# Branch C's pairs prepared on VectorE and ScalarE, with b and k of both heads in the same slots

## The chip, the cores and the metric

The kernel runs on one core of a Trainium2 chip. Its metric is the device time of one execution in microseconds, as the median of several runs. The engines are named as the profile names them: PE (matrix multiply), DVE (VectorE), ACT (ScalarE), POOL (GpSimd) and SP (it issues the DMAs).

## The reference, cut to what matters

A trunk of two layers over 640 tokens (128 context, 512 latent) has three parallel mixers A, B and C. The change touches C alone, a bidirectional delta-rule scan over 8 heads of 64 channels.

```python
def _wkv_scan(s0, r, w, k, v, a_vec, b_vec, reverse):
    def step(state, inp):
        r_t, w_t, k_t, v_t, a_t, b_t = inp
        sa = jnp.einsum('bhij,bhj->bhi', state, a_t)
        state = (state * w_t[:, :, None, :] + sa[..., None] * b_t[:, :, None, :]
                 + v_t[..., None] * k_t[:, :, None, :])
        y_t = jnp.einsum('bhij,bhj->bhi', state, r_t)
        return state, y_t
...
    for d, s0 in ((0, s0_f), (1, s0_b)):
        w_raw = w0[d] + jnp.tanh(wd[:, :, d]) @ w_up[d]
        decay = jnp.exp(-jnp.exp(-jax.nn.softplus(-w_raw) - 0.5))
        a = jax.nn.sigmoid(a0[d] + ad[:, :, d] @ a_up[d])
        k_d = hd(k * (1.0 + (a - 1.0) * k_a))
        s_fin, y_d = _wkv_scan(s0.astype(f32), rh, hd(decay), k_d, vh, -kk, kk * hd(a), reverse=(d == 1))
        bonuses.append(jnp.sum(rh * k_d * r_k, axis=-1, keepdims=True) * vh)
```

## The kernel before

The scan is done in chunks of 64 tokens, ten of them, in two directions. Heads are taken in pairs: a pair p holds 128 channels, head 0 on partitions 0 to 63 and head 1 on partitions 64 to 127, so a layer has four pairs and the kernel eight. A pair goes through these stages:

- `c_prep` (preparation). For each direction d, ACT makes tanh of the decay and of the gate (`lw`, `ta`, line 516), DVE scales the decay (517) and runs its cumulative sum (519), ACT takes exponentials in both signs (`TP`, `TM`, 525), DVE makes `kd` (533, 535) and `b2` (538). Then come eight products, for each head one of each kind on 64 partitions: `b2` times a decay table into `BK` (547, DVE), `kkn` times a table into `L1` (549, DVE), `kd` times a table into `BK` (551, POOL) and `xr` times a table into `L1` (552, POOL). In `BK` the slot of b is the head's number and the slot of k the other one.
- `c_pairs`. PE multiplies `BK` by `L1` of a head for each chunk (`pA`, 611); DVE masks one half of the partitions (614) and ACT copies the other (616), POOL masks that copy (619 to 624). PE then transposes `BK` (`pb`, 631) and ACT copies it back (632).
- `c_inverse`. Sixty small steps on DVE (658, 660) between transposes (652, 662, 670), then small matmuls on PE (`px` 679, `py` 691).
- `c_bonus`, then `c_scan` with ten dependent chunk steps among PE, ACT, DVE and POOL, `c_gn` (a norm per head; its two equal products at 830 stand one on DVE and one on POOL) and `c_out`.

While pair p is scanned, the preparation, the pairs and the inverse of pair p + 1 and the projections of the other mixers ("fillers": matmuls of 320 columns, `pcm`, lines 225 to 227, with weights split into two parts by ACT at 174 and by DVE or POOL at 175) are recorded in between, at a rate from the table `PLAN`. A scheduler then sets the final order of each engine's queue from its own estimate of times, and each engine works through its queue in that order. The transposed `BK` of a pair, `BT` in the scan, is multiplied by `VZ`, in which head 0's values stand on the second half of the partitions and head 1's on the first.

Of the kernel before, what the change touches and what calls it, by code (L numbers as in the profile page):

```python
# [10 lines left out]
F32 = mybir.dt.float32  # L11
# [96 lines left out]
class Trunk:  # L108
    def __init__(self, ctx, tc, I, O):
# [30 lines left out]
        G.memset(self.nhalf, -0.5)  # L140
        self.sc2 = sc = cst.tile([128, KT, 2], F32, tag="sc", name="sc")
# [297 lines left out]
    def c_prep(self, l, p, x, ps):  # L439
# [61 lines left out]
        for d in range(2):  # L501
# [15 lines left out]
            V.tensor_scalar(out=lw, in0=lw, scalar1=-HK, scalar2=-HK, op0=ALU.mult, op1=ALU.add)  # L517
# [10 lines left out]
            else:  # L528
# [4 lines left out]
            V.tensor_scalar(out=kd, in0=ta, scalar1=self.ka2[:, p:p + 1], scalar2=self.ka1[:, p:p + 1],  # L533
                            op0=ALU.mult, op1=ALU.add)
# [5 lines left out]
            def v3(ap, h):  # L540
                return ap[PR[h]].rearrange("p (c s) -> p c s", s=64)


            fl = (slice(None), slice(None, None, -1))[d]
            for h in range(2):
                r_ = PR[h]
                V.scalar_tensor_tensor(out=BK[r_, us, h, fl], in0=v3(b2, h), scalar=0.5,
                                       in1=tB[r_, :, oB:oB + 64], op0=ALU.mult, op1=ALU.mult)
                V.scalar_tensor_tensor(out=L1[h][r_, us, 0, fl], in0=v3(kkn, h), scalar=-1.0,
                                       in1=tA[r_, :, oA:oA + 64], op0=ALU.mult, op1=ALU.mult)  # L550
                G.tensor_tensor(out=BK[r_, us, 1 - h, :], in0=v3(kd, h), in1=tB[r_, :, oB:oB + 64], op=ALU.mult)
                G.tensor_tensor(out=L1[h][r_, us, 1, :], in0=v3(xr, h), in1=tR[r_, :, oR:oR + 64], op=ALU.mult)
# [3 lines left out]
    def c_bonus(self, e, xv, ps):  # L556

        V, S, G, PE = self.V, self.S, self.G, self.PE
        p, cs = e.p, self.cs
        prod = self.tmp("prod")[:, 0:T]  # L560
        G.tensor_tensor(out=prod, in0=e.kds[0], in1=e.kds[1], op=ALU.add)
        V.scalar_tensor_tensor(out=prod, in0=prod, scalar=self.cv[:, CV_RK + p:CV_RK + p + 1], in1=e.xr,
                               op0=ALU.mult, op1=ALU.mult)
        ph, pl = (self.ct.tile([128, 660], F32R, tag="tmp", name=n)[:, 0:T] for n in ("prh", "prl"))
        self.split(ph, pl, prod)
        bonus = self.tmp("bonus")[:, 0:T]
        for half in range(2):
            hs = slice(half * H, half * H + H)
            pb = ps.tile([128, 512], F32, tag="g", name="pbn")
            PE.matmul(pb[:, 0:H], lhsT=self.bones_r, rhs=ph[:, hs], start=True, stop=False)  # L570
            PE.matmul(pb[:, 0:H], lhsT=self.bones_r, rhs=pl[:, hs], start=False, stop=True)
            V.tensor_tensor(out=bonus[:, hs], in0=pb[:, 0:H], in1=xv[:, hs], op=ALU.mult)
        self.nc.sync.dma_start(out=self.bsp[p], in_=bonus)
# [17 lines left out]
    def c_pairs(self, e, ps):  # L591
# [12 lines left out]
        for d in range(2):  # L604
            for h in range(2):
                for c0, n in ((0, 4), (4, 4), (8, 2)):
                    us = slice(10 * d + c0, 10 * d + c0 + n)
                    pA = pc("pA")
                    for j in range(n):
# [4 lines left out]
                    V.tensor_tensor(out=L1[h][QR[h], us].rearrange("p u a s -> p u (a s)"), in0=pv[QR[h]],  # L614
                                    in1=self.amask[QR[h], d:d + 1, :].to_broadcast([64, n, 128]), op=ALU.mult)
                    S.copy(out=AB[PR[h], us], in_=pv[PR[h]].rearrange("p u (a s) -> p u a s", a=2))  # L616
# [11 lines left out]
        for u0 in range(0, 20, 4):  # L628
# [3 lines left out]
            S.copy(out=BK[:, u0:u0 + 4].rearrange("p u a s -> p (u a s)"), in_=pb)  # L632
# [173 lines left out]
    def c_gn(self, l, e):  # L806
# [22 lines left out]
        for x, en in enumerate((V, G)):  # L829
            en.tensor_tensor(out=e.yt[:, :, x], in0=sqy, in1=lnx.to_broadcast([128, 10, 64]), op=ALU.mult)  # L830
# [794 lines left out]
```

## Time and profile before

| what | us |
|---|---|
| median of 3 runs | 2320.77 |
| lowest and highest of them | 2318.45, 2337.36 |
| the profiled execution | 2325.66 |
| its span on the core | 2323.9 |
| PE busy | 2130.8 |
| DVE busy | 1589.3 |
| ACT busy | 1108.1 |
| POOL busy | 690.2 |

The profile is one execution. Its span is what the views cover; 1.8 us of the profiled execution lie around it. An engine's busy time is the union of its instructions' durations; a PE that is busy is not a PE at its peak. A row that gives a mean mixes hindered and unhindered instructions; the least and the median tell them apart.

### The profile page before, as it was taken

Reading aid. Unit: us, or ns where it says so; the run is one execution under the profiler, and the core shown is the slowest. Engines: PE = TensorE matmul, PEld = TensorE weight load, DVE = VectorE, ACT = ScalarE, POOL = GpSimd, SP = SyncE. Lnnn points to the kernel's source line nnn. Section 1 sums busy time; section 2 is a strip of 40 time slices with the busy share of each in tenths; the row PEclk is TensorE's granted clock in tenths of the full one; section 3 lists DMA queues with packets and bytes.
Section 4 is the critical chain, followed back from the end, with each engine's and each line's share of the span. In section 5 each row is a group of like instructions: output and inputs, shape, how many; then the busy total and the mean of one; then the engine's idle time right before and its main releaser. Section 6 shows DMA issues by size and latency. Waiting matters only on the chain.

```text
span 2323.9 us, 40367 instructions
## 1 busy us (share of the span) xinstructions
PE 2130.8 (92%) x15380; PEld 2016.8 (87%) x15380; DVE 1589.3 (68%) x3062; ACT 1108.1 (48%) x2462; POOL 690.2 (30%) x761
## 2 busy tenths in 40 slices
PE   8899998999789889989989999999898889999898
PEld 6889998998789778879988999999898777888898
DVE  4676877867845676775648668668677568667673
ACT  4444443544443666662354444434443447667333
POOL 3332527335233221102033133253352332210011
PEclk9999989989899999999999999899797999999899
DMA  6232222222223311126612322222123231110562
GB/s 227 77 102 77 78 73 95 73 93 84 88 91 109 100 38 52 39 77 192 200 53 74 102 73 79 76 94 76 58 74 99 67 101 46 46 55 24 174 191 83
DMA packets 111762, 209.70 MB, mean 90 GB/s; under 512 B 14416, under 2 KB 33488, under 8 KB 111568
## 3 DMA queue, kind: packets, MB, share of 16 engines
q1 hardware_dynamic: 111568, 207.12, 28.1%
q8 instruction: 121, 1.98, 0.4%
q14 instruction: 73, 0.60, 0.1%
HBM read 163.52 MB, written 43.55 MB: 89 GB/s over the span
## 4 chain that ended last, share of the span: by engine, by line
PE 65%; DVE 18%; ACT 7%; DMA 4%; issue 4%; POOL 2%; DVEq 0%; SPq 0%; ACTq 0%; POOLq 0%
PE pcm L225 10%; PE pcm L226 10%; PE pcm L227 10%; PE sc L958 3%; PE sca L767 2%; PE pm L178 2%; PE pm L179 2%; PE pm L180 2%; DVE wlo L175 2%; PE pA L611 2%; PE pp L973 2%; PE px L679 1%; DVE nm L961 1%; PE scb L782 1%; ACT whi L174 1%
## 5 line engine op out<-in xcount | busy, mean ns | idle before, releaser
L225 PE MATMUL pcm<-hh,whi 128*128 128x320 f32 x1952 | 636.0, 326 | 21.7 <-DVE modc L252 6.7
L227 PE MATMUL pcm<-hh,wlo 128*128 128x320 f32 x1952 | 626.1, 321 | 13.7 <-DVE wlo L175 13.6
L226 PE MATMUL pcm<-hl,whi 128*128 128x320 f32 x1952 | 625.9, 321 | 0.0
L225 PEld LDWEIGHTS pcm<-hh,whi 128*128 128x128 f32 x1952 | 381.3, 195 | 29.4 <-DVE modc L252 7.9
L227 PEld LDWEIGHTS pcm<-hh,wlo 128*128 128x128 f32 x1952 | 380.2, 195 | 18.0 <-DVE wlo L175 16.9
L174 ACT CAST whi<-wraw 128x512 fp32r<-128x512 f32 (+1 forms) x356 | 226.6, 666 | 331.3 <-PE pcm L226 122.0
L226 PEld LDWEIGHTS pcm<-hl,whi 128*128 128x128 f32 x1952 | 381.5, 195 | 1.5
L175 DVE TENSOR_TENSOR wlo<-wraw,whi 128x512 fp32r<-128x512 f32 (+1 forms) x262 | 224.4, 871 | 95.1 <-ACT whi L174 91.3
L175 POOL TENSOR_TENSOR wlo<-wraw,whi 128x512 fp32r<-128x512 f32 x94 | 124.1, 1337 | 195.1 <-ACT whi L174 171.1
L778 POOL COPY ubd<-VZ 64x128 f32<-64x128 f32 x160 | 68.0, 425 | 328.1 <-ACT VZ L775 291.1
L164 DVE TENSOR_TENSOR pl<-pp,ph 128x512 fp32r<-128x512 f32 x160 | 108.4, 685 | 47.8 <-ACT ph L163 46.7
L178 PE MATMUL pm<-yh,whi 128*128 128x320 f32 x384 | 121.7, 317 | 7.1 <-DVE OT L995 3.0
L163 ACT CAST ph<-pp 128x512 fp32r<-128x512 f32 x160 | 92.4, 587 | 64.5 <-PE pp L973 53.9
L961 DVE TENSOR_REDUCE nm<-sc 128x1 f32<-128x640 f32 x128 | 104.4, 818 | 25.0 <-PE sc L958 23.6
L179 PE MATMUL pm<-yl,whi 128*128 128x320 f32 x384 | 121.3, 316 | 0.0
L180 PE MATMUL pm<-yh,wlo 128*128 128x320 f32 x384 | 121.0, 315 | 0.0
L963 ACT ACTIVATE P<-sc,nm 128x640 f32<-128x640 f32 x128 | 102.0, 798 | 18.7 <-DVE nm L961 14.4
L973 PE MATMUL pp<-small,P 128*128 128x128 f32 x640 | 102.2, 280 | 7.2 <-ACT P L963 4.3
L973 PEld LDWEIGHTS pp<-small,P 128*128 128x128 f32 x640 | 80.9, 144 | 24.9 <-ACT P L963 5.3
L611 PE MATMUL pA<-L,BK 128*128 128x128 f32 x640 | 90.7, 285 | 11.4 <-ACT AB L616 7.8
L767 PE MATMUL sca<-VZ,L 128*128 128x64 f32 x640 | 93.3, 285 | 7.7 <-DVE VZ L799 7.6
L996 POOL TENSOR_TENSOR OT<-OT,z 128x640 f32<-128x640 f32 x16 | 27.8, 1736 | 239.7 <-DVE OT L995 216.2
(375 smaller groups left out, 5021.6 us busy)
## 6 DMA issues: line engine op xcount, KB each, us to landing
wraw<-in_win SPq DMA_DIRECT2D x156, 256.0 KB, 2.9
wraw<-in_wg SPq DMA_DIRECT2D x96, 256.0 KB, 3.1
wraw<-in_wmod SPq DMA_DIRECT2D x64, 256.0 KB, 2.9
gsp<-gt SPq DMA_DIRECT2D x48, 320.0 KB, 3.1
gt<-gsp SPq DMA_DIRECT2D x48, 320.0 KB, 3.4
wraw<-in_wo SPq DMA_DIRECT2D x24, 512.0 KB, 4.4
cm<-gsl SPq DMA_DIRECT2D x26, 320.0 KB, 2.5
wraw<-in_wmod SPq DMA_DIRECT2D x16, 512.0 KB, 6.5
```

Of the source, the lines that this page charges most:

```text
L174: self.S.copy(out=hi[part], in_=raw)
L175: sub.tensor_tensor(out=lo[part], in0=raw, in1=f32(hi[part]), op=ALU.subtract)
L178: self.PE.matmul(out, lhsT=lh, rhs=rh, start=first, stop=False)
L179: self.PE.matmul(out, lhsT=lh, rhs=rl, start=False, stop=False)
L180: self.PE.matmul(out, lhsT=ll, rhs=rh, start=False, stop=last)
L225: PE.matmul(p[0:m, 0:H], lhsT=wh[:, kt], rhs=self.hh[:, kt, rs], start=(kt == 0), stop=False)
L226: PE.matmul(p[0:m, 0:H], lhsT=wh[:, kt], rhs=self.hl[:, kt, rs], start=False, stop=False)
L227: PE.matmul(p[0:m, 0:H], lhsT=wl[:, kt], rhs=self.hh[:, kt, rs], start=False, stop=(kt == KT - 1))
L611: PE.matmul(pA[:, j * 128:(j + 1) * 128], lhsT=BK[:, u].rearrange("p a s -> p (a s)"), rhs=L1[h][:, u].rearrange("p a s -> p (a s)"), star ...
L767: PE.matmul(a4[:, d, h], lhsT=L1[h][:, uu[d]].rearrange("p a s -> p (a s)"), rhs=VZ[h][:, cc[d], :], start=(h == 0 and d == 0), stop=False ...
L961: V.tensor_reduce(out=nm, in_=sc[:, :, 0:H], axis=AX.XY, op=ALU.max, negate=True)
L973: PE.transpose(p[:, qt * 128:(qt + 1) * 128], Ps[qt][:, t * 128:(t + 1) * 128], ident)
```

## The change

The four POOL products of a direction go. `kd` and `xr` are multiplied on DVE. In `BK` slot 0 now holds b and slot 1 holds k for both heads, so b and k each take one product on 128 partitions in place of two on 64. The scale and offset of `lw` and of `kd` (before 517 and 533) become ACT activations. In `c_pairs` the halves of `pA` are now the same for both heads, so for head 1 the copies cross partitions. The transposed `BK` needs its halves exchanged for head 1, so the one ACT copy at 632 becomes three: two on ACT and one on DVE. The sum of the two `kd` in `c_bonus` goes from POOL to DVE. In `c_gn` the second, equal product becomes an ACT copy of the first.

```diff
--- before.py
+++ after.py
@@ -138,6 +138,8 @@
         G.memset(self.ones, 1.0)
         self.nhalf = cst.tile([128, 16], F32, tag="nhalf", name="nhalf")
         G.memset(self.nhalf, -0.5)
+        self.nhk = cst.tile([128, 1], F32, tag="nhk", name="nhk")
+        G.memset(self.nhk, -HK)
         self.sc2 = sc = cst.tile([128, KT, 2], F32, tag="sc", name="sc")
         self.S.activation(out=sc, in_=self.cT, func=AF.Tanh, scale=0.5)
         V.scalar_tensor_tensor(out=sc, in0=sc, scalar=1.0, in1=self.cT, op0=ALU.add, op1=ALU.mult)
@@ -514,7 +516,7 @@
                         PE.matmul(pw[:, 0:H], lhsT=wu[j][:, d], rhs=x[:, hs], start=True, stop=True)
                     b0 = 8 * j + d * 4 + p
                     S.activation(out=dst[:, hs], in_=pw[:, 0:H], func=AF.Tanh, scale=0.5, bias=self.wa0[:, b0:b0 + 1])
-            V.tensor_scalar(out=lw, in0=lw, scalar1=-HK, scalar2=-HK, op0=ALU.mult, op1=ALU.add)
+            S.activation(out=lw, in_=lw, func=AF.Identity, scale=-HK, bias=self.nhk)
             c3 = lw.rearrange("p (c s) -> p c s", s=64)
             V.tensor_tensor_scan(out=lw, data0=self.cmask, data1=lw, initial=0.0, op0=ALU.mult, op1=ALU.add)
 
@@ -530,26 +532,25 @@
             V.tensor_copy(out=gm[:, us], in_=TP[:, :, 64])
 
             kd = tmp("kd")[:, 0:T]
-            V.tensor_scalar(out=kd, in0=ta, scalar1=self.ka2[:, p:p + 1], scalar2=self.ka1[:, p:p + 1],
-                            op0=ALU.mult, op1=ALU.add)
+            S.activation(out=kd, in_=ta, func=AF.Identity, scale=self.ka2[:, p:p + 1], bias=self.ka1[:, p:p + 1])
             V.tensor_tensor(out=kd, in0=kd, in1=xk, op=ALU.mult)
             kds.append(kd)
             b2 = ta
             V.scalar_tensor_tensor(out=b2, in0=ta, scalar=1.0, in1=kkn, op0=ALU.add, op1=ALU.mult)
 
-            def v3(ap, h):
-                return ap[PR[h]].rearrange("p (c s) -> p c s", s=64)
+            def v3(ap, r_=slice(0, 128)):
+                return ap[r_].rearrange("p (c s) -> p c s", s=64)
 
 
             fl = (slice(None), slice(None, None, -1))[d]
+            V.scalar_tensor_tensor(out=BK[:, us, 0, fl], in0=v3(b2), scalar=0.5, in1=tB[:, :, oB:oB + 64],
+                                   op0=ALU.mult, op1=ALU.mult)
+            V.tensor_tensor(out=BK[:, us, 1, :], in0=v3(kd), in1=tB[:, :, oB:oB + 64], op=ALU.mult)
             for h in range(2):
                 r_ = PR[h]
-                V.scalar_tensor_tensor(out=BK[r_, us, h, fl], in0=v3(b2, h), scalar=0.5,
-                                       in1=tB[r_, :, oB:oB + 64], op0=ALU.mult, op1=ALU.mult)
-                V.scalar_tensor_tensor(out=L1[h][r_, us, 0, fl], in0=v3(kkn, h), scalar=-1.0,
+                V.scalar_tensor_tensor(out=L1[h][r_, us, 0, fl], in0=v3(kkn, r_), scalar=-1.0,
                                        in1=tA[r_, :, oA:oA + 64], op0=ALU.mult, op1=ALU.mult)
-                G.tensor_tensor(out=BK[r_, us, 1 - h, :], in0=v3(kd, h), in1=tB[r_, :, oB:oB + 64], op=ALU.mult)
-                G.tensor_tensor(out=L1[h][r_, us, 1, :], in0=v3(xr, h), in1=tR[r_, :, oR:oR + 64], op=ALU.mult)
+                V.tensor_tensor(out=L1[h][r_, us, 1, :], in0=v3(xr, r_), in1=tR[r_, :, oR:oR + 64], op=ALU.mult)
 
         return NS(p=p, L1=L1, AB=AB, BK=BK, gm=gm, kds=kds, xr=xr)
 
@@ -558,7 +559,7 @@
         V, S, G, PE = self.V, self.S, self.G, self.PE
         p, cs = e.p, self.cs
         prod = self.tmp("prod")[:, 0:T]
-        G.tensor_tensor(out=prod, in0=e.kds[0], in1=e.kds[1], op=ALU.add)
+        V.tensor_tensor(out=prod, in0=e.kds[0], in1=e.kds[1], op=ALU.add)
         V.scalar_tensor_tensor(out=prod, in0=prod, scalar=self.cv[:, CV_RK + p:CV_RK + p + 1], in1=e.xr,
                                op0=ALU.mult, op1=ALU.mult)
         ph, pl = (self.ct.tile([128, 660], F32R, tag="tmp", name=n)[:, 0:T] for n in ("prh", "prl"))
@@ -611,9 +612,9 @@
                         PE.matmul(pA[:, j * 128:(j + 1) * 128], lhsT=BK[:, u].rearrange("p a s -> p (a s)"),
                                   rhs=L1[h][:, u].rearrange("p a s -> p (a s)"), start=True, stop=True)
                     pv = pA[:, 0:n * 128].rearrange("p (u x) -> p u x", x=128)
-                    V.tensor_tensor(out=L1[h][QR[h], us].rearrange("p u a s -> p u (a s)"), in0=pv[QR[h]],
-                                    in1=self.amask[QR[h], d:d + 1, :].to_broadcast([64, n, 128]), op=ALU.mult)
-                    S.copy(out=AB[PR[h], us], in_=pv[PR[h]].rearrange("p u (a s) -> p u a s", a=2))
+                    V.tensor_tensor(out=L1[h][QR[h], us].rearrange("p u a s -> p u (a s)"), in0=pv[QR[0]],
+                                    in1=self.amask[QR[0], d:d + 1, :].to_broadcast([64, n, 128]), op=ALU.mult)
+                    S.copy(out=AB[PR[h], us], in_=pv[PR[0]].rearrange("p u (a s) -> p u a s", a=2))
                 us = slice(10 * d, 10 * d + 10)
                 if d == 0:
                     G.affine_select(out=AB[PR[h], us], in_=AB[PR[h], us], pattern=[[0, 10], [1, 2], [1, 64]],
@@ -629,7 +630,10 @@
             pb = pc("pb")
             for j in range(4):
                 PE.transpose(pb[:, j * 128:(j + 1) * 128], BK[:, u0 + j].rearrange("p a s -> p (a s)"), ident)
-            S.copy(out=BK[:, u0:u0 + 4].rearrange("p u a s -> p (u a s)"), in_=pb)
+            pv = pb.rearrange("p (u h i) -> p u h i", u=4, h=2)
+            S.copy(out=BK[:, u0:u0 + 4, 0], in_=pv[:, :, 0])
+            S.copy(out=BK[PR[0], u0:u0 + 4, 1], in_=pv[PR[1], :, 1])
+            V.tensor_copy(out=BK[PR[1], u0:u0 + 4, 1], in_=pv[PR[0], :, 1])
 
     def c_inverse(self, e, ps):
 
@@ -826,8 +830,8 @@
         V.tensor_tensor(out=sqy, in0=Y, in1=rs.unsqueeze(2).to_broadcast([128, 10, 64]), op=ALU.mult)
 
         e.yt = e.L1[0].rearrange("p u a s -> p (u a s)")[:, 0:1280].rearrange("p (c x i) -> p c x i", x=2, i=64)
-        for x, en in enumerate((V, G)):
-            en.tensor_tensor(out=e.yt[:, :, x], in0=sqy, in1=lnx.to_broadcast([128, 10, 64]), op=ALU.mult)
+        V.tensor_tensor(out=e.yt[:, :, 0], in0=sqy, in1=lnx.to_broadcast([128, 10, 64]), op=ALU.mult)
+        S.copy(out=e.yt[:, :, 1], in_=e.yt[:, :, 0])
         nc.sync.dma_start(out=e.gz, in_=self.zsp[p])
         nc.sync.dma_start(out=e.bonus, in_=self.bsp[p])
```

The scheduler's order moves with it. The first place is DVE in the preparation of layer 0's first pair, first direction (`lw`, `kd`, `ta`: tiles of the direction; `L_890` and `L_891`, after the change `L_892` and `L_893`: `L1` of head 0 and head 1). Before:

```order
L517 TENSOR_SCALAR lw<-lw 128x640
L519 SCALAR_TENSOR_TENSOR lw<-cmask,lw 128x640
L530 COPY gm<-TP 128x10
L549 SCALAR_TENSOR_TENSOR L_890<-kkn,TP 64x10x64
L549 SCALAR_TENSOR_TENSOR L_891<-kkn,TP 64x10x64
L533 TENSOR_SCALAR kd<-ta,dv 128x640
L535 TENSOR_TENSOR kd<-kd,xk 128x640
L538 SCALAR_TENSOR_TENSOR ta<-ta,kkn 128x640
L547 SCALAR_TENSOR_TENSOR BK<-ta,TM 64x10x64 x2
```

In this piece DVE makes two kinds of product and both scalings; the other two kinds stand on POOL. After the change DVE has at the same place:

```order
L521 SCALAR_TENSOR_TENSOR lw<-cmask,lw 128x640
L532 COPY gm<-TP 128x10
L551 SCALAR_TENSOR_TENSOR L_892<-kkn,TP 64x10x64
L553 TENSOR_TENSOR L_892<-xr,TP 64x10x64
L551 SCALAR_TENSOR_TENSOR L_893<-kkn,TP 64x10x64
L553 TENSOR_TENSOR L_893<-xr,TP 64x10x64
L536 TENSOR_TENSOR kd<-kd,xk 128x640
L539 SCALAR_TENSOR_TENSOR ta<-ta,kkn 128x640
L548 TENSOR_TENSOR BK<-kd,TM 128x10x64
L546 SCALAR_TENSOR_TENSOR BK<-ta,TM 128x10x64
```

Two scalings are gone from the row of instructions, two products of `xr` stand between those of `kkn`, and one product each for k and b closes it.

The second place is DVE where the same pair passes from `c_pairs` to `c_inverse` (`pA`: the products of the pair; `NF`, `LN`: the inverse's tiles). Before:

```order
L614 TENSOR_TENSOR L_891<-pA,amask 64x256
L651 COPY NF<-AB 32x20x32
L652 STREAM_TRANSPOSE LN<-NF 128x1024
L658 TENSOR_TENSOR NF<-LN 128x30
L175 TENSOR_TENSOR wlo<-wraw,whi 128x512
```

Here the inverse opens right behind the last mask. After the change DVE has at the same place:

```order
L177 TENSOR_TENSOR wlo<-wraw,whi 128x512
L636 COPY BK<-pb 64x4x64
L656 STREAM_TRANSPOSE LN<-NF 128x1024
L774 COPY wbd_561<-sca 64x2x64
L636 COPY BK<-pb 64x4x64
L662 TENSOR_TENSOR NF<-LN 128x30
```

Copies of the transposed `BK` now stand on DVE around the transpose that opens the inverse.

## Rows read from the trace of the kernel before

**Rows 1.** The page, part 1: busy us, share of the span, instructions of an engine.
```profile
PE 2130.8 (92%) x15380; PEld 2016.8 (87%) x15380; DVE 1589.3 (68%) x3062; ACT 1108.1 (48%) x2462; POOL 690.2 (30%) x761
```

**Rows 2.** Busy time in the eight preparation stretches: stretch, its length, engines, granted clock, DMA.
```profile
90.00:131.00 41.00, 36.09 (x244) 34.18 (x243) 35.14 (x38) 18.95 (x43) 22.17 (x16) 0.96 0.23 72
222.00:262.00 40.00, 35.85 (x249) 33.00 (x247) 36.13 (x50) 18.31 (x43) 27.43 (x24) 0.91 0.23 70
386.00:406.00 20.00, 14.81 (x108) 14.03 (x107) 17.77 (x17) 7.14 (x16) 17.83 (x15) 0.93 0.25 86
540.00:566.00 26.00, 21.69 (x167) 20.42 (x166) 23.99 (x29) 9.15 (x21) 19.30 (x18) 1.00 0.24 74
1248.00:1275.00 27.00, 22.83 (x136) 20.59 (x136) 25.37 (x25) 11.80 (x28) 14.93 (x10) 0.91 0.21 68
1374.00:1406.00 32.00, 25.80 (x176) 24.12 (x176) 29.79 (x36) 12.22 (x28) 22.70 (x21) 0.95 0.24 75
1553.00:1569.00 16.00, 13.67 (x93) 13.14 (x92) 15.79 (x19) 5.07 (x11) 13.94 (x11) 0.94 0.30 88
1690.00:1706.00 16.00, 12.43 (x90) 11.88 (x88) 15.79 (x15) 5.55 (x13) 13.73 (x11) 1.00 0.25 91
```

**Rows 3.** Chain that ended last, stretch 1374 to 1406: shares by engine and line.
```profile
by line: DVE L L549 20.0%; DVE BK L547 18.8%; issue 16.0%; DVE kd L533 7.0%; DVE wlo L175 6.6%; DVE ta L538 4.9%; DVE kd L535 4.9%; DVE lw L519 4.7%; DVE L L614 4.4%; ACT TP L525 2.4%; ACT whi L174 1.9%; PE pcm L225 1.7%; DVE lw L517 1.6%; 
```

**Rows 4.** PE waits in that stretch: line, releaser, us in total, times, longest.
```profile
PE sca L767 <- DVE VZ L799: 3.7, 1, 3.7
```

**Rows 5.** Timeline of DVE in the third stretch: start, us for all its instructions.
```profile
395.37 4.04 DVE L549 SCALAR_TENSOR_TENSOR L<-kkn,TM 64x640 f32<-64x640 f32 x2
```

**Rows 6.** Timeline of POOL in the same stretch.
```profile
395.18 3.54 POOL L552 TENSOR_TENSOR L<-xr,TM 64x640 f32<-64x640 f32 x2
```

**Rows 7.** DVE groups of the preparation, shapes apart: busy us, mean ns, idle before.
```profile
L549 DVE SCALAR_TENSOR_TENSOR L<-kkn,TM 64x640 f32<-64x640 f32 x16 | 27.2, 1701 | 0.3 <-ACT TM L525 0.2
...
L547 DVE SCALAR_TENSOR_TENSOR BK<-ta,TM 64x640 f32<-64x640 f32 x16 | 24.7, 1541 | 6.0 <-DMA ysp<-BK 5.8
...
L547 DVE SCALAR_TENSOR_TENSOR BK<-ta,TP 64x640 f32<-64x640 f32 x16 | 22.5, 1403 | 0.3
...
L549 DVE SCALAR_TENSOR_TENSOR L<-kkn,TP 64x640 f32<-64x640 f32 x16 | 20.3, 1268 | 0.8 <-PE pyt L843 0.5
...
L535 DVE TENSOR_TENSOR kd<-kd,xk 128x640 f32<-128x640 f32 x16 | 16.5, 1030 | 0.4
...
L538 DVE SCALAR_TENSOR_TENSOR ta<-ta,kkn 128x640 f32<-128x640 f32 x16 | 15.5, 970 | 0.0
...
L533 DVE TENSOR_SCALAR kd<-ta,dv 128x640 f32<-128x640 f32 x16 | 14.2, 888 | 1.7 <-ACT TM L525 0.9 <-ACT ta L516 0.5
...
L517 DVE TENSOR_SCALAR lw<-lw 128x640 f32<-128x640 f32 x16 | 10.2, 634 | 7.4 <-ACT lw L516 7.3
```

**Rows 8.** POOL groups of the products, shapes apart.
```profile
L551 POOL TENSOR_TENSOR BK<-kd,TM 64x640 f32<-64x640 f32 x16 | 30.7, 1921 | 10.9 <-DMA ysp<-BK 3.6 <-ACT ta L516 3.4 <-DVE kd L535 3.3
L551 POOL TENSOR_TENSOR BK<-kd,TP 64x640 f32<-64x640 f32 x16 | 30.2, 1889 | 13.8 <-DVE kd L535 13.3
L552 POOL TENSOR_TENSOR L<-xr,TM 64x640 f32<-64x640 f32 x16 | 30.1, 1880 | 10.9 <-ACT TM L525 7.0 <-ACT wbd L769 3.1
L552 POOL TENSOR_TENSOR L<-xr,TP 64x640 f32<-64x640 f32 x16 | 29.1, 1821 | 14.7 <-ACT TP L525 13.8
```

**Rows 9.** Durations of line 549 in ns, least, median, greatest.
```profile
L549 DVE SCALAR_TENSOR_TENSOR L<-kkn,TP x16: 807/822/2100, 100.0 to 1684.8; 64x640 f32<-64x640 f32 x16
```

**Rows 10.** DVE group of line 614, the 64x256 form, which reads PSUM.
```profile
L614 DVE TENSOR_TENSOR L<-pA,amask 64x256 f32<-64x256 f32 x32 | 13.5, 420 | 13.8 <-PE pA L611 13.4
```

**Rows 11.** ACT group of 128x640 read from SBUF.
```profile
L525 ACT ACTIVATE TP<-lw 128x640 f32<-128x640 f32 x16 | 11.8, 737 | 31.2 <-DVE lw L519 24.3 <-DVE BK L547 6.7
```

**Rows 12.** Timeline of PE at the end of layer 0's last inverse.
```profile
628.51 0.69 PE L679 MATMUL px<-NF,AB 32*32 32x32 f32 x9 [6.03 <-DVE NF L670]
```

## The prediction

> **What bounds the kernel now.** I read the page first: PE is busy for 92% of the span, DVE for 68%, ACT for 48%, POOL for 30% [rows 1]. PE is the engine to keep fed, and a change to the other engines is worth what it takes from PE's idle time. So I looked for the places where PE is idle in branch C, and measured each engine in the eight stretches in which a pair is prepared [rows 2]. There the picture turns round: the stretches are 218 us long together, DVE is busy for 199.8 of them (92%) and PE for 183.2 (84%). PE's idle time is 4.9, 4.2, 5.2, 4.3, 4.2, 6.2, 2.3 and 3.6 us, together 34.8. In the sixth stretch the chain that ended last runs through DVE's lines 549 and 547 for 20.0% and 18.8%, and through other DVE lines for most of the rest [rows 3], and PE's longest wait there is for a DVE result of the scan, which stood in DVE's queue among the products [rows 4]. In preparation DVE is the bound, with POOL beside it.
>
> The reader should then see what slows DVE. In the third stretch DVE's two products of line 549 took 4.04 us while POOL did two of line 552 in 3.54 us [rows 5, 6]. The same instruction has a least duration of 0.81 and a median of 0.82 us in its other form, where it often ran without a POOL product beside it, and a greatest of 2.10 [rows 9]. A DVE product next to a POOL product takes about 2 us instead of 0.82: they take turns. The means of lines 547 and 549 (1.27 to 1.70 us) are mixtures of the two [rows 7].
>
> **The change part by part.**
>
> DVE in the preparation, before: the eight groups add to 27.2 + 24.7 + 22.5 + 20.3 + 16.5 + 15.5 + 14.2 + 10.2 = 151.1 us, that is 18.9 us a pair [rows 7].
>
> After: the two scalings of each direction go to ACT, b takes one product instead of two, k one and r two that are new on DVE, kk keeps two, and the two instructions that make kd and b2 stay. That is 8 a direction and 16 a pair. All have 640 elements a partition; the number of partitions (64 or 128) does not enter, since the 128-partition form of line 538 has a mean of 0.97 us against 1.27 to 1.70 for the 64-partition ones [rows 7]. Unhindered, each costs 0.82 us [rows 9]: 13.1 us a pair. If POOL's other work hindered them as much as it hinders the better form of line 549 now (1.27 us [rows 7]), they would cost 20.3 us. POOL is busy for 152 us in the eight stretches [rows 2] and its four groups of products, which go, for 30.7 + 30.2 + 30.1 + 29.1 = 120.1 us in all [rows 8]; nearly all of it lies in the stretches, so about a fifth of POOL's work there is left (splits of weights, small scan operations). I go a fifth of the way from 13.1 to 20.3: 14.5 us. DVE saves 18.9 - 14.5 = 4.4 us a pair in the preparation; the bounds are a gain of 5.8 and a loss of 1.4.
>
> What that is worth on PE: in a stretch no more than PE's idle time there. The lesser of 4.4 and the idle time, over the eight, is 4.4 + 4.2 + 4.4 + 4.3 + 4.2 + 4.4 + 2.3 + 3.6 = 31.8 us. Part of the idle time is PE waiting for a weight's split behind a DMA or an ACT cast, or for a scan step whose chain is longer than DVE's queue. I take three quarters, an estimate: **24 us**. The bounds are 0 (something else is always just behind) and 31.8.
>
> The clock: the granted clock is 0.91 to 0.96 in six of the stretches [rows 2], so for a part of each PE ran at the lower of its two levels. Length times what is missing to 1.00 is 1.6 + 3.6 + 1.4 + 2.4 + 1.6 + 1.0 = 11.6 us of full-speed work. A denser PE should win back some; I take a third, **4 us**, between 0 and 11.6. The Trainium skill (TensorE: Matmul & The Clock Gate, HAM oscillation — how this bites in real kernels) holds that idle gaps throttle the array and that the slow time is paid on top of the gap; by it all 11.6 us would come back with the gaps. The rows go half with it: the third and the sixth stretch have the most idle time and 0.93 and 0.95, but the fourth has 4.3 us of it at 1.00 [rows 2].
>
> What DVE gets behind the preparation: the sum of the two `kd` (0.82 us unhindered) and five copies of the transposed `BK` out of PSUM, 64x256 each. No DVE copy of that shape is in the trace; the mask of line 614 with the same shape, also out of PSUM, takes 0.42 us [rows 10], and a copy with one input should take no more: 2.1 us for five, with nothing as the lower end if they fall into DVE's idle time. Together 2.9 us a pair at the most. In the order the copies stand around the transpose that opens the inverse, so they lengthen the path to `px`. PE has filler matmuls in front of `px` in most pairs; in layer 0's last pair it has none, and waited 6.03 us for the inverse's last transpose [rows 12]. There, and in the last pair of layer 1, I count half of it, **2 us of cost** over both (0 to 6), as the preparation ahead of them is 4.4 us shorter.
>
> ACT: the scalings of `lw` and `kd` are 32 activations of 128x640 at 0.74 us [rows 11], 23.6 us; the copy of the equal product in the norm 8 at 0.74, 5.9 us; one more copy for each transposed group, at most 40 times 0.42, 17 us. ACT goes from 48% to about 50% busy [rows 1]. The cover is its idle half; I cost it at nothing. If the cover is gone the path of the decay gets 0.74 - 0.63 = 0.11 us longer for each of 16 directions [rows 7, 11], 1.7 us. No engine change is added there, since tanh already runs on ACT. The DVE copy is a new wait in DVE's queue: it waits for PE's transposes, and if the three copies of a group go one after another, for ACT's two as well. Behind it stand the inverse's small steps, and behind those PE's `px`; that is the path on which the cost above is counted. On POOL the masks of `AB` and the scan's copies no longer stand behind products of 1.8 to 1.9 us [rows 8], which I count at nothing. SP's queue has the same DMAs.
>
> The sum is -24 - 4 + 2 = -26 us. Against the profiled execution (2325.7 us, 1.8 of them outside the span) that is 2299.7; that execution lies 4.9 us above the median of the runs, so I forecast 2320.8 - 26 = **2295 us**, 1.1% faster.
>
> **The rivals.**
>
> *A, the work only changes its owner (about 2312 us).* DVE and POOL took turns, so a product moved to DVE still takes DVE's time; only merging and the scalings win. Then the 4.4 us of the preparation are paid back by the 2.9 us behind it, as DVE has no slack in the whole of a pair: 1.5 us a pair, 12 in all, three quarters of it on PE, -9 us. For it: DVE's share of the stretches [rows 2]. Against it: in the inverse PE mostly has fillers and the copies are hidden. The Trainium skill (Perfetto Trace Analysis, Optimizing Scalar/DVE Operations) warns of this: GpSimd and DVE share a read port, so moving work between the two may not help. The trace agrees that they take turns [rows 5, 6], but it also shows a price: two DVE and two POOL products took 4.04 us, and four unhindered on DVE would take 3.28, and for b and k, merged, two would take 1.64. The same case, little change, holds if PE's order has no room: PE is at 92% and its waits turn up at other places.
>
> *B, slower (about 2355 us).* DVE's queue becomes the longer one. POOL's splits move up into the time that its products leave and hinder DVE's 16 instructions as much as now, 1.27 us each. Then a pair loses 1.4 us in the preparation and 2.9 behind it, 4.3 us, 34 us over eight pairs, since DVE is busy for 92% of these stretches and PE waits for it. It decides from the point at which the mean of DVE's products stays above 18.9 / 16 = 1.18 us. Against it: only about a fifth of POOL's work in these stretches is left [rows 2, 8].
>
> *C, a bigger gain (about 2272 us).* All 31.8 us of idle time and the whole 11.6 us of clock come back, and the shorter preparation lets the last pair's inverse end earlier, 6 us [rows 12]: 49 us. For it: DVE's lines fill most of the chain there [rows 3], so a DVE that is a quarter quicker could feed PE without a gap. Against it: stretches two and five have POOL at little more than half busy and yet the same idle time [rows 2].
>
> **How the numbers follow.** The forecast (-14 to -38 us) has a chance of 0.50, A 0.25, B 0.10, C 0.15. About 1% (23 us, below 2297.6 or above 2344.0) is what a measurement of this kernel can tell from no change. The forecast's upper part, 0.32 of 0.50, and C lie beyond it: faster 0.47. The rest of the forecast, A and a little of B are within it: 0.44. Slower: 0.09. For the range I leave out the lower part of C and all of B with the worst of A: 2268 to 2322.
>
> **What would show it.** In the profile after, the mean of DVE's products in the preparation should be 0.8 to 1.0 us, POOL should fall by the 120 us and by 16 more instructions of about 1.9 us (the sum of the `kd` and the norm's product) to some 540 us busy, and DVE by 8 times 4.4 - 2.9 us, and by what its other instructions were hindered, to 1550 to 1580; PE's idle time in the preparation stretches should fall from 35 to 10 to 15 us, with a clock nearer 1.00. B would show as means above 1.18 us. A would show as PE's idle time moved to `px` and to the scan's steps. I am wrong if the products run unhindered and PE's idle time in branch C does not fall: then DVE was not what held PE.

## The result and the profile after

The changed kernel has a median of 2295.1 us (2283.91 to 2301.3, 4 runs) against 2320.28 us before (4 runs): a ratio of 0.986, 95% interval 0.982 to 0.99. A later series of the same kernel gave 2288.5 us and 0.9837 (0.981 to 0.9864). The forecast was 2295. Its profiled execution took 2299.7 us with a span of 2298.0, 25.9 us less than before.

The page, part 1, of the changed kernel:

```profile
PE 2125.8 (93%) x15380; PEld 2015.1 (88%) x15380; DVE 1551.2 (68%) x3110; ACT 1145.5 (50%) x2542; POOL 535.0 (23%) x682
```

Against [rows 1], POOL falls by 155 us (forecast: to 540), DVE by 38 (forecast: to 1550 to 1580), and ACT grows by 37.

The eight preparation stretches of the changed kernel, chosen by the same work as [rows 2] (stretch, length, PE, weight loads, DVE, ACT, POOL, granted clock, DMA):

```profile
95.00:131.00 36.00, 34.54 (x250) 33.59 (x249) 27.22 (x39) 23.53 (x50) 7.03 (x9) 1.00 0.29 96
225.00:262.00 37.00, 35.68 (x281) 34.38 (x281) 31.11 (x56) 23.79 (x52) 10.48 (x18) 1.00 0.27 88
395.00:415.00 20.00, 19.25 (x149) 18.44 (x148) 17.60 (x28) 9.93 (x22) 7.11 (x9) 1.00 0.30 99
532.00:558.00 26.00, 23.30 (x178) 22.23 (x177) 22.62 (x34) 11.85 (x26) 8.54 (x10) 1.00 0.29 99
1240.00:1267.00 27.00, 27.00 (x192) 26.60 (x191) 22.13 (x31) 17.05 (x37) 2.46 (x4) 1.00 0.31 100
1356.00:1388.00 32.00, 30.02 (x224) 28.85 (x223) 29.05 (x47) 19.76 (x41) 8.22 (x13) 1.00 0.25 80
1531.00:1547.00 16.00, 16.00 (x122) 16.00 (x121) 14.52 (x24) 8.76 (x18) 2.29 (x6) 1.00 0.34 117
1668.00:1684.00 16.00, 15.57 (x116) 15.38 (x115) 13.77 (x24) 7.52 (x16) 3.28 (x6) 1.00 0.26 95
sum 210.00, PE 201.35 PEld 195.47 DVE 178.03 ACT 122.19 POOL 49.42; mean PE 25.17 PEld 24.43 DVE 22.25 ACT 15.27 POOL 6.18
```

PE's idle time there is 8.7 us in 210 where it was 34.8 in 218, the clock is 1.00 in all eight where six were at 0.91 to 0.96, and POOL is busy for 49 us in place of 152.

DVE's groups of the preparation and the new copies, by form (busy us, mean ns, idle before), which answer to [rows 7] and [rows 10]:

```profile
L636 DVE COPY BK<-pb 64x256 f32<-64x256 f32 x40 | 16.7, 417 | 1.2
...
L539 DVE SCALAR_TENSOR_TENSOR ta<-ta,kkn 128x640 f32<-128x640 f32 x16 | 15.5, 969 | 0.0
...
L553 DVE TENSOR_TENSOR L<-xr,TM 64x640 f32<-64x640 f32 x16 | 14.4, 899 | 0.0
...
L551 DVE SCALAR_TENSOR_TENSOR L<-kkn,TM 64x640 f32<-64x640 f32 x16 | 14.1, 882 | 2.6 <-ACT TM L527 2.5
...
L546 DVE SCALAR_TENSOR_TENSOR BK<-ta,TP 128x640 f32<-128x640 f32 x8 | 6.5, 817 | 0.0
...
L548 DVE TENSOR_TENSOR BK<-kd,TM 128x640 f32<-128x640 f32 x8 | 6.5, 816 | 0.0
```

Together with the groups that aren't shown, the 128 instructions of the preparation that answer to [rows 7] take 110.9 us, a mean of 0.87 us, where those of [rows 7] add to 151.1.

To see where the time went I cut the whole of branch C at three marks: the first cumulative sum of the decay (519, now 521), the transpose that opens the inverse (652, now 656) and the first `px` (679, now 683). The sums over the pairs, from windows between these marks, are:

| part | before | after | difference |
|---|---|---|---|
| preparation and pairs, 8 | 537.7 | 502.6 | -35.1 |
| PE idle in it | 39.7 | 10.6 | -29.1 |
| clock missing to 1.00, times length | 16.5 | 0.0 | -16.5 |
| inverse, 8 | 334.8 | 358.7 | +23.9 |
| PE idle in it | 32.9 | 42.2 | +9.3 |
| clock missing to 1.00, times length | 9.1 | 16.9 | +7.8 |
| from `px` to the next preparation, 6 | 190.1 | 176.5 | -13.6 |
| PE idle in it | 4.1 | 4.1 | 0.0 |
| clock missing to 1.00, times length | 33.6 | 42.3 | +8.7 |

The rest of the span differs in length by 1.1 us. Idle time and missing clock, added, are what PE lost: 56.2 to 10.6 us in the preparation and 42.0 to 59.1 in the inverse, 98.2 to 69.7 in these two. Their 28.5 us less are near the 25.9 that the span lost, but they aren't the whole account, since 8.7 us of clock were lost in addition behind `px`, so the three stages lost 19.8 us less. Over the whole span PE's idle time fell from 193.1 to 172.2 us (span less busy time) and the missing clock, in windows of 20 us, from 135.6 to 130.6: together the 25.9. The 13.6 us behind `px` are a shift of work: 362 filler matmuls of 320 columns run there instead of 505, the rest elsewhere. The third of these six stretches, before and after:

```profile
478.70:513.00 34.30, 33.51 (x338) 32.99 (x338) 19.23 (x38) 14.57 (x41) 12.67 (x18) 0.85 0.24 75
```

```profile
480.70:510.50 29.80, 29.79 (x293) 29.09 (x294) 17.18 (x39) 13.97 (x37) 10.43 (x16) 0.71 0.13 40
```

PE is hardly idle there, yet its granted clock is 0.85 and then 0.71. The windows of the eight inverse stretches after, the fourth and the sum:

```profile
574.00:618.90 44.90, 38.16 (x283) 36.09 (x281) 40.27 (x99) 21.21 (x52) 11.38 (x20) 0.96 0.35 115
...
sum 358.70, PE 316.54 PEld 308.21 DVE 325.44 ACT 161.74 POOL 55.16; mean PE 39.57 PEld 38.53 DVE 40.68 ACT 20.22 POOL 6.90
```

PE's waits in the whole span, the row of `px` (us in all, count, longest):

```profile
PE px L683 <- DVE NF L674: 19.3, 4, 10.2
```

The wait at `px` is 19.3 us; the same line of the kernel before had 8.3 for this releaser (6.03 of them in [rows 12]) and 6.7 for another.

### The profile page after: what moved, and what is told of

The parts are those of the page before. It is cut to its first block, busy times and chain, and to the rows that moved or that the text cites. A ratio compares the mean times of both kernels' runs of the same rounds, so it can differ in the third digit from the quotient of the medians.

```text
span 2298.0 us, 40440 instructions
## 1 busy us (share of the span) xinstructions
PE 2125.8 (93%) x15380; PEld 2015.1 (88%) x15380; DVE 1551.2 (68%) x3110; ACT 1145.5 (50%) x2542; POOL 535.0 (23%) x682
## 4 chain that ended last, share of the span: by engine, by line
PE 69%; DVE 14%; ACT 8%; issue 4%; DMA 3%; POOL 1%; DVEq 0%; SPq 0%; ACTq 0%; POOLq 0%
PE pcm L227 11%; PE pcm L228 10%; PE pcm L229 10%; PE sc L962 3%; PE pA L612 3%; PE pm L180 3%; PE pm L181 3%; PE pm L182 2%; PE sca L771 2%; PE pp L977 2%; PE scb L786 1%; DVE LN L664 1%; DVE NF L662 1%; PE pout L180 1%; PE pout L181 1%
## 5 line engine op out<-in xcount | busy, mean ns | idle before, releaser
L177 DVE TENSOR_TENSOR wlo<-wraw,whi 128x512 fp32r<-128x512 f32 (+1 forms) x262 | 208.7, 810 | 88.8 <-ACT whi L176 87.1
L782 POOL COPY ubd<-VZ 64x128 f32<-64x128 f32 x160 | 63.1, 395 | 415.8 <-ACT VZ L779 360.8
L967 ACT ACTIVATE P<-sc,nm 128x640 f32<-128x640 f32 x128 | 101.8, 797 | 15.7 <-DVE nm L965 11.6
L771 PEld LDWEIGHTS sca<-VZ,L 128*128 128x128 f32 x640 | 93.5, 214 | 6.0 <-DVE VZ L803 4.4
L662 DVE TENSOR_TENSOR NF<-LN 128x30 f32<-128x30 f32 (+14 forms) x240 | 84.5, 352 | 6.6
```

Source lines behind the costliest of these rows:

```text
L177: sub.tensor_tensor(out=lo[part], in0=raw, in1=f32(hi[part]), op=ALU.subtract)
L662: V.tensor_tensor(out=pv_, in0=LNv[:, s + 1:32, s:s + 1].to_broadcast([128, m, s]), in1=LNv[:, s:s + 1, 0:s].to_broadcast([128, m, s]), op ...
L771: PE.matmul(a4[:, d, h], lhsT=L1[h][:, uu[d]].rearrange("p a s -> p (a s)"), rhs=VZ[h][:, cc[d], :], start=(h == 0 and d == 0), stop=False ...
```

## The experiments

Theory 1 says that DVE and POOL take turns and that the end of this is the gain. Theory 2 says that DVE's own smaller count of work is the gain. Ratios are to the kernel before, with 95% intervals. Its median was 2320.3 us in the series of the result and 2322.8 (e1 to e4), 2324.7 (e5 to e8) and 2326.2 (the rest) in the others, so kernels of different series are compared by their ratios, times 2323; the changed kernel is 0.9837 to 0.986. Prep and inverse are the lengths of the table above, from each run's trace, and "PE lost" is PE's idle time and missing clock in these two stages, worked out as there (before: 537.7, 334.8 and 98.2; changed, first series: 502.6, 358.7 and 69.7).

| run | median us | ratio | prep | inverse | PE lost |
|---|---|---|---|---|---|
| changed, second series | 2288.5 | 0.9837 (0.981 to 0.9864) | 503.4 | 361.3 | 74.3 |
| e1 products on POOL | 2297.9 | 0.9894 (0.9867 to 0.992) | 507.3 | 361.9 | 80.9 |
| e2 extra POOL products | 2329.5 | 1.003 (1.0014 to 1.0046) | 547.2 | 355.5 | 114.9 |
| e3 scalings alone | 2305.0 | 0.9915 (0.9886 to 0.9944) | 518.2 | 341.9 | 88.3 |
| e4 slots alone | 2323.2 | 0.9995 (0.997 to 1.0019) | 524.9 | 359.5 | 98.4 |
| e5 third copy on ACT | 2277.9 | 0.9801 (0.978 to 0.9823) | 508.9 | 337.1 | 62.6 |
| e6 splits on DVE | 2284.3 | 0.9836 (0.9817 to 0.9855) | 496.5 | 360.0 | 60.8 |
| e7 another order | 2287.5 | 0.9842 (0.9817 to 0.9868) | 501.7 | 357.7 | 66.7 |
| e8 ACT copies for products | 2279.2 | 0.9812 (0.9796 to 0.9829) | 496.3 | 336.0 | 55.1 |
| e9 = e5 and e6 | 2276.2 | 0.9779 (0.9751 to 0.9806) | 500.3 | 336.9 | 54.8 |
| e10 unmerged on DVE | 2305.4 | 0.9914 (0.989 to 0.9938) | 534.8 | 330.5 | 75.3 |
| e11 three copies on DVE | 2295.0 | 0.9867 (0.984 to 0.9894) | 487.5 | 395.5 | 77.9 |

In ten of the thirteen (these and the first series) the change of "PE lost" against before is within 10 us of what the ratio says, in e5 and e11 within 11, and in the changed kernel's second series 14 off. So these two stages show where most of a change sits, but not its last 10 us.

**Is it the turns?** Two runs change POOL alone, or take its products away without giving DVE anything. e2 adds POOL products to the changed kernel:

```diff
+                G.tensor_tensor(out=scr[r_], in0=v3(kd, r_), in1=tB[r_, :, oB:oB + 64], op=ALU.mult)
+                G.tensor_tensor(out=scr[r_], in0=v3(xr, r_), in1=tR[r_, :, oR:oR + 64], op=ALU.mult)
```

> The changed kernel with four extra POOL products a direction into a tile that nothing reads, 64 in all; DVE, ACT and PE have the same instructions. Theory 1: POOL's extra products hinder DVE's, whose mean goes from 0.86 to above 1.2 us, and the preparation gets longer by 3 to 6 us a pair: 2315 to 2340 us. Theory 2: POOL has room (23% busy), so nothing waits for these products: 2285 to 2302 us.

It lost the whole gain. The page of e2, part 1:

```profile
PE 2124.6 (91%) x15380; PEld 2012.9 (87%) x15380; DVE 1609.2 (69%) x3110; ACT 1142.8 (49%) x2542; POOL 658.3 (28%) x746
```

DVE has the same 3110 instructions as in the changed kernel and is busy for 58 us longer. Two DVE groups of e2, by form:

```profile
L547 DVE SCALAR_TENSOR_TENSOR BK<-ta,TP 128x640 f32<-128x640 f32 x8 | 12.8, 1595 | 0.1
...
L549 DVE TENSOR_TENSOR BK<-kd,TM 128x640 f32<-128x640 f32 x8 | 11.9, 1484 | 0.1
```

The added group on POOL, in the same view:

```profile
L555 POOL TENSOR_TENSOR scr<-kd,TM 64x640 f32<-64x640 f32 x16 | 32.1, 2004 | 27.9 <-DVE kd L537 27.1
```

The sum row of e2's eight preparation stretches:

```profile
sum 547.20, PE 509.64 PEld 495.55 DVE 419.12 ACT 278.45 POOL 291.17; mean PE 63.70 PEld 61.94 DVE 52.39 ACT 34.81 POOL 36.40
```

The two DVE products shown have means of 1.60 and 1.48 us beside POOL's and 0.82 in the changed kernel. Only the four groups of products into `BK` are held up this much (1.33 to 1.60 us); those into `L1` stay at 0.82 to 0.94, so the mean over the 128 instructions is 1.03, below the 1.2 that I had expected. DVE's splits of the weights (175, now 177) take 18.6 of the 58 us. PE is idle for 37.6 of 547.2 us and the clock lost 17.5, as before the change. 64 POOL products cost 0.017 to 0.0193 times 2323, 39 to 45 us, 0.6 to 0.7 us each. In e8 the products go and ACT copies stand in their place:

```diff
-                G.tensor_tensor(out=BK[r_, us, 1 - h, :], in0=v3(kd, h), in1=tB[r_, :, oB:oB + 64], op=ALU.mult)
-                G.tensor_tensor(out=L1[h][r_, us, 1, :], in0=v3(xr, h), in1=tR[r_, :, oR:oR + 64], op=ALU.mult)
+                S.copy(out=BK[r_, us, 1 - h, :], in_=v3(kd, h))
+                S.copy(out=L1[h][r_, us, 1, :], in_=v3(xr, h))
```

> The kernel before with POOL's 64 products of the preparation replaced by ACT copies of kd and xr; the multiplication by the decay tables is left out, so that DVE gets nothing in their place. Theory 1: the whole hindrance goes and DVE keeps its 64-partition products at 0.82 us, ACT gets 64 times 0.7 = 45 us: as good as the change or better, 2280 to 2300 us. Theory 2: DVE's instruction count is that of before, so no gain: 2312 to 2330 us.

The page of e8, part 1:

```profile
PE 2107.8 (93%) x15380; PEld 1999.6 (88%) x15380; DVE 1538.2 (68%) x3062; ACT 1153.4 (51%) x2526; POOL 567.1 (25%) x697
```

At least as good as the change (the intervals overlap), with DVE's 3062 instructions as before. Both runs speak for theory 1: the hindrance is real, and worth up to 44 us when its end adds nothing to DVE (0.0188 times 2323). It is an upper bound, because the copies don't wait for the decay tables as the products did [rows 8]; what that is worth was not run.

**Does moving the products win it?** e1 puts them back on POOL in the changed kernel, and e10 moves them to DVE without merging.

```diff
-            V.tensor_tensor(out=BK[:, us, 1, :], in0=v3(kd), in1=tB[:, :, oB:oB + 64], op=ALU.mult)
+            G.tensor_tensor(out=BK[:, us, 1, :], in0=v3(kd), in1=tB[:, :, oB:oB + 64], op=ALU.mult)
-                V.tensor_tensor(out=L1[h][r_, us, 1, :], in0=v3(xr, r_), in1=tR[r_, :, oR:oR + 64], op=ALU.mult)
+                G.tensor_tensor(out=L1[h][r_, us, 1, :], in0=v3(xr, r_), in1=tR[r_, :, oR:oR + 64], op=ALU.mult)
```

> The changed kernel with the products of kd and xr back on POOL; the merged b and k, the scalings on ACT and the three copies stay. Theory 1 (DVE and POOL take turns, and the gain is the end of that): DVE has 6 products a pair fewer of its own, but they are hindered again, mean of the b and kk products 1.3 to 1.7 us, the time goes back to 2308 to 2325 us. Theory 2 (the gain is DVE's own smaller count, from merging b and from the scalings on ACT): DVE's work is smaller still than in the changed kernel, so 2280 to 2297 us.

> The kernel before with everything of the change but the new slots: the scalings on ACT, all products on DVE with 64 partitions each (20 instructions a pair instead of 16), the sum of kd on DVE, the norm's copy on ACT; one ACT copy of the transposed BK as before, none on DVE. If the DVE copies cost what the merging saves: preparation about 3.3 us a pair longer than after the change (525 to 530 us in sum), inverse 335 to 342 us, 2285 to 2300 us in all, the same as the change. If the copies cost nothing on the way to px: 2305 to 2320 us.

e1 lost 0.0034 to 0.0057, 8 to 13 us (its interval overlaps that of the first series and not that of the second). The b and kk products are hindered again, with a mean of 1.29 us, but the median is well below theory 1's range and at the edge of theory 2's. The edit of e10, to the kernel before, with e3's scalings and the change's sum and norm beside it:

```diff
-G.tensor_tensor(out=BK[r_, us, 1 - h, :], in0=v3(kd, h), in1=tB[r_, :, oB:oB + 64], op=ALU.mult)
+V.tensor_tensor(out=BK[r_, us, 1 - h, :], in0=v3(kd, h), in1=tB[r_, :, oB:oB + 64], op=ALU.mult)
-G.tensor_tensor(out=L1[h][r_, us, 1, :], in0=v3(xr, h), in1=tR[r_, :, oR:oR + 64], op=ALU.mult)
+V.tensor_tensor(out=L1[h][r_, us, 1, :], in0=v3(xr, h), in1=tR[r_, :, oR:oR + 64], op=ALU.mult)
```

e10 equals e3, which has the scalings alone. So moving 64 unmerged products from POOL to DVE won nothing that can be told: what the turns had cost, DVE now spends itself. From e1 to the changed kernel 48 products move, none of them merged on the way, and win 8 to 13 us. So the move by itself won 0 and 8 to 13 us in the two comparisons; in the first the sum of `kd` and the norm's copy moved with it. The preparation of e10 is 31 to 32 us longer than the changed kernel's, near the price of 32 more products of 0.88 us, 28 us. PE is idle for 17.2 us of it, where e3 has 36.3, but for 41.6 us of the inverse, where e3 has 27.2.

**The other parts alone.** e3 has the scalings of the change in the kernel before:

```diff
-V.tensor_scalar(out=lw, in0=lw, scalar1=-HK, scalar2=-HK, op0=ALU.mult, op1=ALU.add)
+S.activation(out=lw, in_=lw, func=AF.Identity, scale=-HK, bias=self.nhk)
-V.tensor_scalar(out=kd, in0=ta, scalar1=self.ka2[:, p:p + 1], scalar2=self.ka1[:, p:p + 1],
-                op0=ALU.mult, op1=ALU.add)
+S.activation(out=kd, in_=ta, func=AF.Identity, scale=self.ka2[:, p:p + 1], bias=self.ka1[:, p:p + 1])
```

e4 is the changed kernel with those two lines, the sum of kd and the norm's halves as before, and the products on POOL by e1's edit, so that of the change only the slots are left.

> The kernel before with the two scalings of a direction on ACT, and nothing else changed. Theory 1: DVE loses 24 us of busy time, of which about 9 us were waits for POOL that the next DVE instruction takes over; 2305 to 2320 us. Theory 2: the scalings are about a third of the saving: 2308 to 2314 us. This run sizes a part and does not tell the theories apart by itself.

> The kernel before with the new slots alone: b merged on DVE, k merged on POOL, the three copies of the transposed BK; the xr products, the sum of kd and the second norm product stay on POOL, the scalings on DVE. Theory 1: POOL's products go from 64 to 48 and DVE's from 64 to 48 in the preparation, so half of the effect of the whole change, less the copies' 2 us a pair: 2305 to 2320 us, with means of DVE's products still above 1.2 us. Theory 2: two thirds of the saving: 2300 to 2308 us.

The scalings gave 20 us (0.85%), near the 24.4 us that they took on DVE. The slots gave nothing in sum: the preparation 13 us shorter, the inverse 25 longer. With e1's 8 to 13 us for the move these parts add to 29 to 34 us, against 32 to 38 for the whole change by its ratios. So over half of the gain came with POOL's products still in place, and theory 2 has its share.

**The copies.** All kernels with one copy of the transposed `BK` on DVE have an inverse of 355 to 362 us, all without it 330 to 342. e5 moves that copy to ACT, e11 moves the other two to DVE.

```diff
-            V.tensor_copy(out=BK[PR[1], u0:u0 + 4, 1], in_=pv[PR[0], :, 1])
+            S.copy(out=BK[PR[1], u0:u0 + 4, 1], in_=pv[PR[0], :, 1])
```

> The changed kernel with the third copy of the transposed BK on ACT instead of DVE. After the change the time from the transpose that opens the inverse to px grew by 23.9 us over eight pairs. Theory A (the copies on DVE stand in the inverse's way): DVE loses 16.7 us, the inverse gets 1.5 to 3 us shorter a pair, 2278 to 2290 us. Theory B (the inverse is longer for another reason: splits that the scheduler moved into it, or POOL's splits beside its small steps): no change, 2290 to 2300 us, with the inverse as long as after the change.

> The changed kernel with all three copies of the transposed BK on DVE (80 more DVE instructions of 256 elements, 33 us). If copies on DVE lengthen the inverse one for one: inverse stretches 380 to 395 us in sum instead of 358, and 2305 to 2325 us in all. If one copy's cost was an accident of the order: inverse as after the change, 2288 to 2302 us.

The sum rows of the inverse stretches of e5 and then of e11:

```profile
sum 337.20, PE 301.40 PEld 294.19 DVE 301.08 ACT 166.45 POOL 49.12; mean PE 37.67 PEld 36.77 DVE 37.63 ACT 20.81 POOL 6.14
```

```profile
sum 395.60, PE 344.30 PEld 335.11 DVE 361.38 ACT 150.64 POOL 58.75; mean PE 43.04 PEld 41.89 DVE 45.17 ACT 18.83 POOL 7.34
```

With none, one and three copies the inverse takes 337, 359 to 361 and 396 us. The differences are more than the copies' own time, since 40 of them are 16.7 us. The kernel's time does not follow, as PE fills most of the longer stage with fillers (344 of 396 us busy in e11), and e11 is at most 7 us slower than the changed kernel; my range for it was wrong. By the medians e5 is 8 to 14 us faster than the changed kernel, though the intervals overlap a little: in its inverse PE is idle for 35.8 us and the clock lost 13.3, together 49 where the changed kernel has 59 to 63. That is not at `px`, where e5 still waits 18.0 us, but spread over the stage. The copies are not all of it either: e10, with none of them on DVE and the shortest inverse of all, has PE idle for 41.6 us there and loses 53.3 with the clock, where the kernel before loses 42.0.

**Order and splits.** e7 writes the two products into `BK` behind the four into `L1`, with no other edit:

```diff
-            V.scalar_tensor_tensor(out=BK[:, us, 0, fl], in0=v3(b2), scalar=0.5, in1=tB[:, :, oB:oB + 64],
-                                   op0=ALU.mult, op1=ALU.mult)
-            V.tensor_tensor(out=BK[:, us, 1, :], in0=v3(kd), in1=tB[:, :, oB:oB + 64], op=ALU.mult)
             for h in range(2):
...
+            V.scalar_tensor_tensor(out=BK[:, us, 0, fl], in0=v3(b2), scalar=0.5, in1=tB[:, :, oB:oB + 64],
+                                   op0=ALU.mult, op1=ALU.mult)
+            V.tensor_tensor(out=BK[:, us, 1, :], in0=v3(kd), in1=tB[:, :, oB:oB + 64], op=ALU.mult)
```

e6 has the next edit at both calls of `modulation`, and e9 is e5 and e6 together.

```diff
-                        yield from self.modulation(*m, wp, ps, self.G)
+                        yield from self.modulation(*m, wp, ps, self.V)
```

> The changed kernel with the two products into BK written behind those into L1 in the source; the same instructions in another order. It shows what an order alone can move. Both theories: within 8 us of the changed kernel, 2287 to 2303 us; if it moves by more than 15 us, no difference of that size between two of these kernels says anything about its mechanism.

> The changed kernel with the splits of the modulation's weights on DVE instead of POOL (94 of 512 columns). POOL then has no product of two tiles beside the preparation or the inverse apart from small scan operations. Theory 1: DVE gets 94 times 0.69 = 65 us of work and is freed of what these splits hinder, at about one turn of 1 us for each that meets DVE; the two cancel about: 2285 to 2310 us, and the inverse's small steps show no instruction above 0.8 us. Theory 2 (counts alone matter): 65 us more on DVE, 2310 to 2335 us.

> The changed kernel with both of two edits that were run singly: the third copy of the transposed BK on ACT and the modulation's splits on DVE. Each alone came out 4 to 17 us below the changed kernel. If the copies cost by standing in the inverse, and the splits by hindering DVE: 2265 to 2278 us, the inverse stretches at 335 to 345 us in sum. If DVE is the bound by its count alone, the 44 us of splits cost more than they free: 2278 to 2295 us.

The order alone moved the time by no more than two series of the same kernel differ. The splits on DVE changed nothing that can be told from the noise; POOL kept 30 of the 94. e9 is the fastest, below the changed kernel's interval in the same series; that it beats e5 is not shown. The changed kernel repeated:

> The changed kernel unaltered, for a comparison on the same chip: 2285 to 2302 us by every theory.

## Why the prediction was right, point by point

The sum was right, and some of its terms were off in opposite ways, so that the forecast's closeness to the median (2295 and 2295.1 us) is partly luck; the second series has 2288.5.

*What bounds.* Right: DVE, with POOL beside it, held PE in the preparation. e2 restores PE's idle time and the low clock there with POOL's products alone. The reading of [rows 9] was loose: a product of 0.82 us need not be one without POOL beside it. Four of these began 0.02 to 0.03 us ahead of a POOL product of line 552, which then took 2.08 us and more; the one that comes second waits.

*DVE in the preparation.* I had 4.4 us saved a pair, from 18.9 to 14.5. Measured: 151.1 to 110.9 us, 5.0 a pair. The share of POOL's work that I left in the stretches was too small: the products took 104 of the 152 us there, not nearly all of their 120, so a third is left and not a fifth (49 us after the change). It hindered less than I let it, with a mean of 0.87 us. The mechanism needs a correction too. Of the 40 us, 24.4 are the two scalings that went to ACT. Beyond the scalings (e3) the move of the products is worth nothing by itself (e10), the slots with their merging 5 us by themselves (e1), and both together 13 to 18 (the changed kernel, 17 below e10 in the same series), with the three copies paid for. So the products win by leaving POOL and being merged at once, not by either alone.

*What it is worth on PE.* I took three quarters of 31.8, 24 us, and 4 of the 11.6 us of clock, 28 together. In the stretches of [rows 2], 26 of 34.8 us of idle time went, and all of the clock's loss; over whole preparations 29.1 and 16.5. The idle term was right, and with the 2 us of cost it is also right for the kernel: 22 us forecast, 20.9 measured over the span. The clock term was too small for the preparation, but the kernel kept none of that: the inverse lost 7.8 us more of clock (12.5 in the second series), and the stretches behind `px` 8.7 more, which is all of the 16.5. The whole span's 5.0 us are no support for my 4, since in the second series its missing clock is 135.7 us, as before the change. On the preparation the Trainium skill (TensorE: Matmul & The Clock Gate, HAM oscillation — how this bites in real kernels) was nearer than my third: the clock was lost with the gaps and came back with them. Behind `px` the trace goes another way: 4.1 us of idle time in 190, and 33.6 us of clock lost. Without POOL's products the preparation loses 0 to 4.8 us of clock, and with them 9.0 to 18.8.

*The copies and the sum of kd.* I had a DVE time of 2.9 us a pair, and a cost of 2 us for the whole kernel. DVE spent 16.7 us on the copies and 7.2 on the sum, 3.0 a pair, so the duration was right. 15.5 us of the copies lie in the inverse, as I said; the sum lies in the preparation and not on the way to `px`. The cost was mis-sized: I let it count at `px` in two pairs, and PE lost 17.1 us more over all eight inverses, of which the copies are a part: moving one of the three to ACT is worth 8 to 14 us, and e10 loses 53.3 us in the inverse without them. Part of what this term lost, the preparation's larger gain covered; that is the luck.

*ACT at nothing.* Right as far as shown: ACT took 37 us more (48% to 50%), and e5, with more still, was faster.

*The rivals.* A's core, that moved work only changes its owner, is what e10 shows for unmerged products; it did not decide because the products were merged and the scalings left DVE. Its sign, idle time moved to `px` and to the scan, came in part: `px` waits 19.3 us where it waited 15.0, and behind `px` the idle time stayed at 4.1. B did not come: DVE's mean is 0.87 us, below its 1.18. C came nearly true in the preparation (45.6 us of idle time and clock) and was paid back in part in the inverse (17.1) and behind `px` (8.7 of clock). Of the two stretches named against it, the second has POOL busy for 27.4 of 40 us, not little more than half; the first (22.2 of 41) fits the words.

Not settled: how much of e5's gain is the copy and how much the new order of fillers that comes with it. Any edit moves the scheduler's order, and the two series of the changed kernel differ by 5 us in their ratios.

## What to carry to other kernels

Where two engines take turns, moving work from one to the other wins little by itself (0 us here, and 8 to 13 where the products were merged already). What won was to move work to a third engine (20 us), and to merge and move at once (13 to 18). Price the turns by adding work that nothing reads on the suspected engine, as e2 does. Add up PE's idle time and its missing clock over every stage to the end of the span, since a stage's gain can be lost again in the next ones, in gaps and in clock.

## What was not expected of the hardware

A DVE instruction of 10 columns waits as well: the copy of `gm` (line 530) took 0.16 us at the least and 1.52 at the most in the kernel before, the longest beside a POOL product (line 830). And a DVE product that reads PSUM and one tile of SBUF (line 614) never did, at 0.70 us at the most for 512 columns, though a POOL product ran beside some of them all the way (at 116.4 and 121.5 us).
